# Retention's gates half by block products, retention in fewer VectorE instructions with its normalization a chunk later, and the order of the attention values' weight sums

## The chip, the cores and the metric

The kernel runs on one core of a Trainium2 chip. A core has a matrix engine (TensorE, PE in the profile; its weight loads are listed apart as PEld), VectorE (DVE), ScalarE (ACT), GpSimd (POOL) and SyncE (SP), which here only issues transfers. Each engine works through its own instructions in order; semaphores hold an instruction until what it needs is there. The metric is the device time of one execution in microseconds (us); of several runs the median counts.

## The reference

One decoder block on a sequence of 1024 tokens with 1024 channels, in float32. `h = modulate(rms_norm(x))` is projected by `w_in` to the queries, keys, values and gates of a retention branch (4 heads, 256 wide for queries and keys, 512 for values and gates), to the queries, keys and values of three groups of dilated attention, and to two merge gates. Retention goes through each head in chunks of 128 tokens:

```python
s = jnp.einsum('bhid,bhjd->bhij', qi, ki) * inner_decay[None]
o = (jnp.einsum('bhij,bhje->bhie', s, vi)
     + jnp.einsum('bhid,bhde->bhie', qi, state) * q_decay[None, :, :, None])
state = (state * chunk_decay[None, :, None, None]
         + jnp.einsum('bhjd,bhje->bhde', ki * k_decay[None, :, :, None], vi))
...
ro = ((ro - mu) * lax.rsqrt(var + GN_EPS)).transpose(0, 2, 1, 3).reshape(B, S, RET_V_W)
ro = (ro * gn_g.astype(jnp.float32) + gn_b.astype(jnp.float32)).astype(h.dtype)
ret_out = (jax.nn.silu(rg) * ro) @ w_ret_out
```

Then come the attention, the gated merge, `w_o`, a squared-ReLU MLP and a last norm. Six modulation vectors are made from `c` by `w_ada`.

## The kernel before, in words

**Arithmetic.** Each float32 operand is split into a high part (`hi`, a cast on ACT) and a low part (`lo`, the rest, a subtraction on DVE), and a product is three matmuls: low by high, high by low, high by high (`mm3`, L201, L203, L205). A full matmul has 128 x 128 weights and 512 moving columns.

**Plain and block products.** A plain projection of 128 output channels (`proj_mm`) goes over 8 blocks of input channels, 2 halves of the tokens and 3 matmuls: 48. A block product (`Blocks`, and by hand in `avb_mm` and `v_mm`) takes 256 output channels, both halves of the tokens and all input channels as a 2 x 2 matrix of blocks and needs seven products in place of eight, at the price of sums of weights and of results on DVE (L243, L1043) and copies on ACT. One such pair has 7 x 4 x 3 = 84 matmuls.

**Order of the work.** The order on every engine is the order in which the Python code issues (`manual_schedule`). Stages: the norm of the input; the attention's values (`av_first`, plain, and `av_blocks`, block products; its table `work` says what is issued behind which product); 18 pairs of block products (`queries_keys`, order `PAIRS`: r = retention's queries or keys, a = attention's queries, g = merge gates); retention's values (`values`, block products); retention; the attention of two pairs of heads; the merge; the MLP.

**Attention values' sums.** The sums s1, s2 and s4 of the weights are made in place in two tiles `AB["s", j]` by accumulating transfers that POOL issues (`avb_add`, L886). `avb_split` splits such a tile (ACT L914, DVE L916 or L918) and then issues the next sum into it. `avb_post` takes results out of PSUM (ACT L948, L951). `bias_out` (L440) spreads the attention's bias rows in DRAM, twelve stores on SP.

**Retention.** `chunk(h, c)` is called for 4 heads x 8 chunks (g = 8h + c) and does, in this order:
- SP fetches the queries, keys and values of chunk g + 3 (`fetch`).
- PE: the state's update `kv`, two tiles of 512 columns (not in chunk 7); then a part of the gate projection `rg` (16 blocks of 48 matmuls in the 32 chunks: 24 matmuls a chunk, 12 here and 12 below).
- DVE: state = state x decay + kv (L698; a copy, L696, in chunk 0), in two halves.
- `ahead(2)`: what the next chunk's loads need: a split of gate weights before every second chunk (ACT L191, DVE L192) and in every chunk one product of `w_ada` with c (DVE L452, L454), 32 in all.
- `s_kt(g + 1)`: PE makes the scores `sT` of the next chunk and transposes its keys; ACT L635 and DVE L636, L637 make `sm`, ACT L638 and DVE L639 split it, ACT L645 and DVE L646 make `kh` and `kl`, the keys for the next `kv`.
- PE: `o`, from the state's halves `sh`, `sl` (6 matmuls, not in chunk 0) and from scores and values (3).
- ACT L711 and DVE L712: the new state's halves, 512 columns at a time; ACT L612 and POOL L613 split queries and keys of chunk g + 2.
- PE: `on_T(g - 1)`, four transposes of the normalized output of the chunk before, which ACT (L658) copies out; the rest of the gate matmuls.
- DVE L722, L723, L724, POOL L725 (a power of -1/2), DVE L726, L728: mean, variance, and the normalized `o`.
- ACT L732, every second chunk: Silu of a gate block. In chunks 0 to 3, `u_final` finishes one block of 128 channels of the head before: ACT L667 twice, DVE L669 once, a store on SP.

[...]

Of the kernel before, what the change touches and what calls it, by code (L numbers as in the profile page):

```python
# [21 lines left out]
H = 4  # L22
# [18 lines left out]
CS_QD = 132  # L41
CS_QD2 = 136
# [92 lines left out]
def block_kernel(ctx, tc, io, stop=None, dbg=None):  # L135
# [535 lines left out]

    def chunk(h, c, ahead, w=None):
# [12 lines left out]
        kvs = []  # L685
# [8 lines left out]
        for i, kv in enumerate(kvs):  # L694
            if c == 0:
                nc.vector.tensor_copy(st[:, i, :], kv)  # L696
            else:
                nc.vector.scalar_tensor_tensor(st[:, i, :], st[:, i, :], float(GAMMA[h] ** C), kv,  # L698
                                               op0=ALU.mult, op1=ALU.add)
        ahead(2)  # L700
        if g + 1 < NG:
            s_kt(g + 1)
        po = ps_s(f"o{h}{c}")
# [5 lines left out]
        if c < NC - 1:  # L709
            for i in range(2):  # L710
                nc.scalar.copy(sh[:, i, :], st[:, i, :])  # L711
                nc.vector.tensor_sub(sl[:, i, :], st[:, i, :], fv(sh[:, i, :]))  # L712
# [11 lines left out]
        nc.vector.tensor_scalar(gr, ba[:, 1:2], ct[:, CS_QD2 + h:CS_QD2 + h + 1], GN_EPS, op0=ALU.mult, op1=ALU.add)  # L724
        nc.gpsimd.tensor_tensor(gr, gr, mhalf[:, 0:1], op=ALU.pow)  # L725
        nc.vector.tensor_mul(gr, gr, ct[:, CS_QD + h:CS_QD + h + 1])  # L726
        on = p.tile([P, DV], F32, tag="on", bufs=1, name=f"onm{h}{c}")
        nc.vector.tensor_scalar(on, po, ba[:, 0:1], gr, op0=ALU.subtract, op1=ALU.mult)  # L728
# [138 lines left out]
    def avb_tile(n, part, name):  # L867

        if n in (2, 6) or n > 11:
            return x4(name, F32R)  # L870
# [94 lines left out]
    def av_blocks(ahead):  # L965

        def tables():
# [32 lines left out]
    PAIRS = [{"r": r_pairs, "a": a_pairs, "g": g_pairs}[i].pop(0) for i in "rargrargrargrargaa"]  # L1000
# [3 lines left out]
    def a_load(q, part):  # L1004
        pair = PAIRS[q]
        src = io[{"g": "w_gate2", "a": "w_aq"}.get(pair[0]) or f"w_r{pair[1]}"]
# [19 lines left out]
    def a_out(q, n, x, y=None):  # L1026
# [12 lines left out]
        f = AF.Sigmoid if pair[0] == "g" else AF.Copy  # L1039
        if y is None:  # L1040
            nc.scalar.activation(o, view(x), f)
        else:
            (nc.vector.tensor_add if n == "12" else nc.vector.tensor_sub)(o, view(x), view(y))  # L1043
            if pair[0] == "g":
                nc.scalar.activation(o, o, f)
        if n in ("12", "21"):
            if pair[0] == "g":
                dst = gate_d[GATES[2 * pair[1] + i]]
            elif pair[0] == "a":
# [19 lines left out]

    gate_d = [dram.tile([P, S], F32, name=f"gated{i}") for i in range(16)]  # L1070
# [109 lines left out]

    def values(ahead):
# [1387 lines left out]
```

## Time and profile before

| | |
|---|---|
| median of 3 runs | 2232.15 us (2231.87 to 2234.04) |
| profiled execution | 2236.08 us |
| its span, first to last instruction | 2234.3 us |
| granted TensorE clock, mean | 0.993 |
| chain that ended last, PE's share | 86% |

The profile is of one execution. "Busy" is the time in which an engine had an instruction at work; PE's busy time is modelled, since matmuls are pipelined, so the distance between starts says more than a duration. The view of stretches gives the busy time of each engine in a window with the granted clock; the view of waits says which instruction waited, for whom, how long and how often; the timeline lists starts and durations, with the wait before an instruction and what ended it in brackets.

### The profile page before, as it was taken

How to read it: one execution, taken by the hardware profiler on the slowest of the kernel's cores; microseconds unless marked ns; L12 is line 12 of the kernel's file. 1: busy time of each engine (PE TensorE's matmuls, PEld its weight loads, DVE VectorE, ACT ScalarE, POOL GpSimd, SP SyncE). 2: the span in 40 equal slices, each digit the busy share in tenths (PEclk: the TensorE clock that was granted, in tenths of full speed). 3: DMA queues.
4: the chain of work that ended last, by engine and by line, in shares of the span. 5: the costliest groups of instructions: out<-in, count | busy, mean ns of one | idle time of the engine just before them, and what ended most of it. 6: DMA issues, size and time to landing. Idle time of an engine off the chain costs nothing.

```text
span 2234.3 us, 27105 instructions
## 1 busy us (share of the span) xinstructions
PE 2173.9 (97%) x10082; PEld 1799.7 (81%) x10082; DVE 1469.6 (66%) x2303; ACT 912.2 (41%) x1671; POOL 155.1 (7%) x176
## 2 busy tenths in 40 slices
PE   7999999999999999999999999999999999999998
PEld 5778888888877888888888788888778888788887
DVE  6657777754448778855554654676866665787845
ACT  4432332223334445544634633524444445433412
POOL 0100111000012122110000000002000000000003
PEclk9999999999999999999999999999999999999999
DMA  9859999724775556549723355654234444745322
GB/s 384 248 174 284 288 306 270 205 87 174 250 270 170 166 181 207 193 159 249 228 62 96 102 210 195 235 179 160 66 133 150 156 155 164 257 144 170 123 85 76
DMA packets 157602, 414.15 MB, mean 185 GB/s; under 512 B 27222, under 2 KB 55133, under 8 KB 153054
## 3 DMA queue, kind: packets, MB, share of 16 engines
q1 hardware_dynamic: 149598, 364.19, 46.6%
q0 software_dynamic: 7872, 48.24, 9.3%
q8 instruction: 79, 1.29, 0.2%
q14 instruction: 53, 0.43, 0.1%
HBM read 321.51 MB, written 156.13 MB: 214 GB/s over the span
## 4 chain that ended last, share of the span: by engine, by line
PE 86%; DVE 5%; ACT 2%; issue 1%; DMA 1%; POOL 0%; POOLq 0%; SPq 0%; DVEq 0%; ACTq 0%
PE qap L203 5%; PE qap L205 5%; PE qap L201 5%; PE fp L201 4%; PE fp L203 4%; PE fp L205 4%; PE rg L201 3%; PE rg L203 3%; PE rg L205 3%; PE f2a L203 2%; PE f2a L205 2%; PE f2a L201 2%; PE ak L201 2%; PE ak L203 2%; PE ak L205 2%; PE va L203 1%
## 5 line engine op out<-in xcount | busy, mean ns | idle before, releaser
L201 PE MATMUL qap<-hh,qaw 128*128 128x512 f32 x216 | 84.0, 389 | 0.0
L203 PE MATMUL qap<-hl,qaw 128*128 128x512 f32 x216 | 84.0, 389 | 0.0
L205 PE MATMUL qap<-hh,qaw 128*128 128x512 f32 x216 | 84.0, 389 | 0.0
L613 POOL TENSOR_TENSOR j<-qk,j 128x512 fp32r<-128x512 f32 x32 | 43.3, 1354 | 468.4 <-ACT j L612 446.4
L2028 ACT ACTIVATE a<-a 128x512 f32<-128x512 f32 x48 | 30.3, 632 | 79.5 <-DVE a L2027 79.5
L1925 POOL TENSOR_TENSOR accnf<-accnf,sqnf 128x256 f32<-128x256 f32 (+1 forms) x18 | 16.6, 921 | 620.7 <-ACT sqnf L1924 620.7
L1382 ACT ACTIVATE P<-P,ng 128x128 f32<-128x128 f32 (+1 forms) x96 | 41.9, 438 | 38.7 <-DVE ng L1379 38.7
L258 DVE TENSOR_TENSOR fw<-w1r,fw 128x512 fp32r<-128x512 f32 x48 | 33.0, 688 | 36.2 <-ACT fw L248 36.2
L2214 ACT CAST w2h<-w2s 128x512 fp32r<-128x512 f32 x36 | 22.4, 621 | 78.8 <-DVE w2s L2252 77.7
L635 ACT COPY sm<-sT 128x128 f32<-128x128 f32 x32 | 8.5, 265 | 103.9 <-PE sT L626 103.9
L201 PE MATMUL fp<-h2h,fw 128*128 128x512 f32 x128 | 50.0, 390 | 0.0
L203 PE MATMUL fp<-h2l,fw 128*128 128x512 f32 x128 | 49.8, 389 | 0.0
L205 PE MATMUL fp<-h2h,fw 128*128 128x512 f32 x128 | 49.8, 389 | 0.0
L201 PE MATMUL roa<-rh,rwl 128*128 128x512 f32 x128 | 49.8, 389 | 0.0
L203 PE MATMUL roa<-rl,rwh 128*128 128x512 f32 x128 | 49.8, 389 | 0.0
L205 PE MATMUL roa<-rh,rwh 128*128 128x512 f32 x128 | 49.8, 389 | 0.0
L1763 DVE TENSOR_TENSOR rwl<-rwl,rwh 128x1024 fp32r<-128x1024 f32 x25 | 30.2, 1220 | 29.1 <-ACT rwh L1793 29.1
L1925 POOL TENSOR_TENSOR accn<-accn,sqn 128x512 f32<-128x512 f32 x12 | 15.5, 1293 | 478.2 <-ACT sqn L1924 478.2
L201 PEld LDWEIGHTS qap<-hh,qaw 128*128 128x128 f32 x216 | 40.5, 188 | 8.5
L203 PEld LDWEIGHTS qap<-hl,qaw 128*128 128x128 f32 x216 | 40.6, 188 | 8.4
L205 PEld LDWEIGHTS qap<-hh,qaw 128*128 128x128 f32 x216 | 40.6, 188 | 8.3
L258 DVE TENSOR_TENSOR qaw<-wa,qaw 128x512 fp32r<-128x512 f32 x54 | 36.9, 685 | 7.5 <-ACT qaw L248 7.5
(3063 smaller groups left out, 7197.1 us busy)
## 6 DMA issues: line engine op xcount, KB each, us to landing
v<-vd SPq DMA_DIRECT2D x32, 512.0 KB, 4.8
raw<-in_w_ada_dram SPq DMA_DIRECT2D x32, 512.0 KB, 5.1
w1r<-in_w_ff_dram SPq DMA_DIRECT2D x32, 512.0 KB, 5.0
vd<-vo SPq DMA_DIRECT2D x24, 512.0 KB, 4.2
yt<-y POOLq DMA_DIRECT2D x6, 2048.0 KB, 15.4
xsd<-as SPq DMA_DIRECT2D x24, 512.0 KB, 2.8
w2r<-in_w_ff2s_dram SPq DMA_DIRECT2D x24, 512.0 KB, 7.1
em<-in_w_ada_dram SPq DMA_DIRECT2D x16, 512.0 KB, 10.2
```

What stands on the lines that cost most here:

```text
L201: nc.tensor.matmul(o, wl, xh, start=first, stop=False, skip_group_check=skip)
L203: nc.tensor.matmul(o, wh, xl, start=False, stop=False, skip_group_check=skip)
L205: nc.tensor.matmul(o, wh, xh, start=False, stop=last, skip_group_check=skip)
L258: nc.vector.tensor_sub(t[:, 512:], src, fv(t[:, :512]))
L613: nc.gpsimd.tensor_sub(t[:, 1], src, fv(t[:, 0]))
L635: nc.scalar.copy(sm, ps[:, :C])
L1382: nc.scalar.activation(v, v, AF.Exp, bias=ng[:, blk:blk + 1], accum_out=st[:, g, blk, 2 + a:3 + a])
L1763: nc.vector.tensor_sub(lo, fv(lo), fv(hi))
L1925: (nc.vector if f == 7 else nc.gpsimd).tensor_add(G["acc", key], G["acc", key], sq)
L2028: nc.scalar.activation(o, o, AF.Relu)
L2214: nc.scalar.copy(hi, src)
```

## The change: what it does

1. Of each head's four gate blocks two are still projected inside retention (12 matmuls a chunk); the other two are a pair of block products among the `queries_keys` pairs (s in `PAIRS`, now 22 pairs, the merge gates last), with Silu, stored to DRAM (`srg_d`) and fetched in chunks 4 and 5.
2. In retention, `kv` is one double tile and the state's update, high and low half are one instruction each on 1024 columns. The query decay is taken out of the normalization (its epsilon is scaled by a table), and `o` is normalized by ACT with a scale and a bias, one chunk later (`normed(g - 1)`, behind `s_kt`). The transposes come two chunks later than `o` and stand between the gate matmuls and the scores. `u_final` moves to chunks 2 to 5.
3. Thirteen of the 32 `w_ada` products move from retention to `values` (`v_mod`).
4. In `av_blocks` the splits of s1 stand one to two products earlier, the first in tiles of another ring, and `bias_out` moves to `queries_keys`.

```diff
+    def normed(g):
+
+        h, c = divmod(g, NC)
+        po, ba, gr = hd["o", h, c]
+        nb = R["p"].tile([P, 1], F32, tag="nb", bufs=2, name=f"nb{h}{c}")
+        nc.vector.scalar_tensor_tensor(nb, ba[:, 0:1], -1.0, gr, op0=ALU.mult, op1=ALU.mult)
+        on = R["p"].tile([P, DV], F32, tag="on", bufs=2, name=f"onm{h}{c}")
+        nc.scalar.activation(on, po, AF.Identity, scale=gr, bias=nb)
+        hd["o", h, c] = on
...
-        if c % 2 == 0:
+        if c % 4 == 0:
             hd["rgw"] = w
             hd["rgp"] = ps_mm(f"rg{h}{c}")
-        ks = range(4 * (c % 2), 4 * (c % 2) + 4)
+        if c in (4, 5):
+            hd["srg", h, c - 2] = etile(f"srg{h}{c - 2}")
+            nc.sync.dma_start(hd["srg", h, c - 2], srg_d[h][c - 4])
+        ks = range(2 * (c % 4), 2 * (c % 4) + 2)
...
+            kv = ps_mm(f"kv{h}{c}")
             for i in range(2):
-                kv = ps_s(f"kv{h}{c}{i}")
-                mm3([kv], (kh[:, i, :], kl[:, i, :]), [(vh, vl)], True, True)
-                kvs.append(kv)
+                mm3([kv[:, i]], (kh[:, i, :], kl[:, i, :]), [(vh, vl)], True, True)
         if g > 0:
-            proj_mm(hd["rgp"], hd["rgw"], ks[:2])
...
+            proj_mm(hd["rgp"], hd["rgw"], ks[:1])
+        if g > 1:
+            on_T(*divmod(g - 2, NC))
+        if c == 0:
+            nc.vector.tensor_copy(flat(st), flat(kv))
+        elif c < NC - 1:
+            nc.vector.scalar_tensor_tensor(flat(st), flat(st), float(GAMMA[h] ** C), flat(kv),
+                                           op0=ALU.mult, op1=ALU.add)
         ahead(2)
         if g + 1 < NG:
             s_kt(g + 1)
+        if g > 0:
+            normed(g - 1)
         po = ps_s(f"o{h}{c}")
...
-            for i in range(2):
-                nc.scalar.copy(sh[:, i, :], st[:, i, :])
-                nc.vector.tensor_sub(sl[:, i, :], st[:, i, :], fv(sh[:, i, :]))
+            nc.scalar.copy(flat(sh), flat(st))
+            nc.vector.tensor_sub(flat(sl), flat(st), fv(flat(sh)))
         if g + 2 < NG:
             jit_qk(g + 2)
         if g > 0:
-            on_T(*divmod(g - 1, NC))
-        if g > 0:
-            proj_mm(hd["rgp"], hd["rgw"], ks[2:])
+            proj_mm(hd["rgp"], hd["rgw"], ks[1:])
...
-        nc.vector.tensor_scalar(gr, ba[:, 1:2], ct[:, CS_QD2 + h:CS_QD2 + h + 1], GN_EPS, op0=ALU.mult, op1=ALU.add)
+        nc.vector.tensor_add(gr, ba[:, 1:2], ct[:, CS_EPS + h:CS_EPS + h + 1])
         nc.gpsimd.tensor_tensor(gr, gr, mhalf[:, 0:1], op=ALU.pow)
-        nc.vector.tensor_mul(gr, gr, ct[:, CS_QD + h:CS_QD + h + 1])
-        on = p.tile([P, DV], F32, tag="on", bufs=1, name=f"onm{h}{c}")
-        nc.vector.tensor_scalar(on, po, ba[:, 0:1], gr, op0=ALU.subtract, op1=ALU.mult)
-        hd["o", h, c] = on
-        if c % 2 == 1:
-            hd["srg", h, c // 2] = etile(f"srg{h}{c // 2}")
-            nc.scalar.activation(hd["srg", h, c // 2], flat(hd["rgp"]), AF.Silu)
-        if h > 0 and c < 4:
-            u_final(h - 1, (c,))
+        hd["o", h, c] = po, ba, gr
+        if c % 4 == 3:
+            hd["srg", h, c // 4] = etile(f"srg{h}{c // 4}")
+            nc.scalar.activation(hd["srg", h, c // 4], flat(hd["rgp"]), AF.Silu)
+        if h > 0 and 1 < c < 6:
+            u_final(h - 1, (c - 2,))
...
-        if n in (2, 6) or n > 11:
+        if n in (2, 4, 6) or n > 11:
             return x4(name, F32R)
...
-                (0, 1): [lambda: sums_of_h("t1")], (0, 2): [lambda: bias_out(0)],
-                (0, 3): [lambda: sums_of_h("t3"), lambda: bias_out(1)],
-                (1, 0): [lambda: avb_split(2, 0), lambda: bias_out(2)], (1, 1): [lambda: avb_split(2, 1)],
+                (0, 1): [lambda: sums_of_h("t1")], (0, 2): [lambda: avb_split(2, 0)],
+                (0, 3): [lambda: sums_of_h("t3")], (1, 0): [lambda: avb_split(2, 1)],
...
-    PAIRS = [{"r": r_pairs, "a": a_pairs, "g": g_pairs}[i].pop(0) for i in "rargrargrargrargaa"]
+    s_pairs = [("s", h) for h in range(H)]
+    PAIRS = [{"r": r_pairs, "a": a_pairs, "g": g_pairs, "s": s_pairs}[i].pop(0) for i in "rsrarsrarsrarsraggagga"]
...
-            if pair[0] == "g":
+            if pair[0] in "gs":
                 nc.scalar.activation(o, o, f)
...
+            if n == "11" and 0 < q < 4:
+                bias_out(q - 1)
...
+    def v_mod(i):
+
+        t, j = cs[:, i % 2], VMODS[i]
+        nc.vector.scalar_tensor_tensor(t, t, 1.0, cb, op0=ALU.mult, op1=ALU.mult, accum_out=mods[:, j:j + 1])
+        nc.vector.tensor_add(mods[:, j:j + 1], mods[:, j:j + 1], vec[:, VC_BADA + j:VC_BADA + j + 1])
...
+            if i < last:
+                nc.sync.dma_start(cs[:, i % 2], io["w_ada"][VMODS[i]])
...
+                if p == 3 and i > 0:
+                    v_mod(i - 1)
...
-                      ([wsplit(io["w_rg"][4 * h + c // 2])] if c % 2 == 0 else []) + [mod_load(later_mods[8 * h + c])],
-                      manual=True)
+                      ([wsplit(io["w_rg"][2 * h + c // 4])] if c % 4 == 0 else []) +
+                      ([mod_load(later_mods.pop(0))] if c in ((1, 2, 3, 5, 6) if h < 3 else (1, 3, 5, 6)) else []), manual=True)
...
+                normed(NG - 1)
                 for _ in range(4):
                     next(gen)
+                on_T(H - 1, NC - 2)
                 on_T(H - 1, NC - 1)
```

More of the change, by code (lines that the diff above doesn't have):

```diff
@@ L40 @@
 CS_KDEC = 128
-CS_QD = 132
-CS_QD2 = 136
+CS_EPS = 132
 CS_ONE = 140
@@ L1038, in a_out @@
             view = lambda z: z.rearrange("p (i r) -> p r i", r=8)
-        f = AF.Sigmoid if pair[0] == "g" else AF.Copy
+        f = {"g": AF.Sigmoid, "s": AF.Silu}.get(pair[0], AF.Copy)
         if y is None:
@@ L1048, in a_out @@
                 dst = gate_d[GATES[2 * pair[1] + i]]
+            elif pair[0] == "s":
+                dst = srg_d[pair[1]][i]
             elif pair[0] == "a":
@@ L1068, in rotate @@
             nc.sync.dma_start(qk_d[h][:, 2 * (t == "k") + i], OA[q][i])
+    srg_d = [[dram.tile([P, S], F32, name=f"srgd{h}{i}") for i in range(2)] for h in range(H)]
     gate_d = [dram.tile([P, S], F32, name=f"gated{i}") for i in range(16)]
@@ L1179, in v_post @@
         nc.sync.dma_start(v_d[2 * hp + int(blk[0]) - 1][:, p + 4 * (int(blk[1]) - 1)], fv(t))
+    later_mods = [G1 + k for k in range(NK)] + [SH2 + k for k in range(NK)] + \
+                 [SC2 + k for k in range(NK)] + [G2 + k for k in range(NK)]
+    def v_mod(i):
+        t, j = cs[:, i % 2], VMODS[i]
+        nc.vector.scalar_tensor_tensor(t, t, 1.0, cb, op0=ALU.mult, op1=ALU.mult, accum_out=mods[:, j:j + 1])
+        nc.vector.tensor_add(mods[:, j:j + 1], mods[:, j:j + 1], vec[:, VC_BADA + j:VC_BADA + j + 1])
+    VMODS = [later_mods.pop(0) for _ in range(len(VSEQ) - 1)]
     def values(ahead):
@@ L1223, in block_kernel @@
     steps.add(queries_keys, manual=True)
-    later_mods = [G1 + k for k in range(NK)] + [SH2 + k for k in range(NK)] + \
-                 [SC2 + k for k in range(NK)] + [G2 + k for k in range(NK)]
     for h in range(H):
```

16 lines of the change are left out of this document (5 added, 11 removed).

## The prediction, made before the change was run

> **What bounds the kernel now.** I began with the shares of the page: TensorE (PE) is at work nearly all the time, so a change pays only if it takes matmuls away or ends one of PE's few waits, and it costs as soon as it gives PE a new one.
>
> ```profile
> span 2234.3 us, 27105 instructions
> PE 2173.9 (97%) x10082; PEld 1799.7 (81%) x10082; DVE 1469.6 (66%) x2303; ACT 912.2 (41%) x1671; POOL 155.1 (7%) x176
> ```
>
> Next the view by stretches for the stages that the edits touch: the queries, keys and gates by block products (158.8 to 501.5 us), the values (to 657.8) and retention (to 976.7). The first three columns are the stretch, its length and PE's busy time with its instructions; VectorE (DVE) stands fourth after the length's PE and PEld.
>
> ```profile
> 158.80:501.50 342.70, 342.70 (x1514) 283.85 (x1512) 244.29 (x383) 100.18 (x171) 33.65 (x48) 1.00 0.78 243
> 501.50:657.80 156.30, 154.23 (x674) 127.23 (x672) 73.28 (x87) 60.15 (x84) 7.11 (x10) 0.99 0.62 219
> 657.80:976.70 318.90, 313.12 (x1510) 259.79 (x1509) 247.82 (x519) 142.68 (x359) 57.91 (x62) 0.99 0.55 183
> ```
>
> In the block products PE never stops: 342.70/1512 = 0.2267 us a matmul of 512 columns. In retention it stops only at the start; the view of waits has two PE rows there:
>
> ```profile
> PE rg L201 <- DVE kl L646: 3.3, 1, 3.3
> PE kv L201 <- DVE kl L646: 2.5, 1, 2.5
> ```
>
> So retention's 32 chunks are bound by PE, and the next question is how closely DVE follows. The timeline of DVE for one round of a chunk that also finishes a block of the head before (starts, durations):
>
> ```profile
> 767.42 1.28 DVE L698 SCALAR_TENSOR_TENSOR state<-state,kv 128x512 f32<-128x512 f32 x2
> 768.62 1.22 DVE L452 SCALAR_TENSOR_TENSOR raw<-raw,cb 128x1024 f32<-128x1024 f32 x1
> ...
> 769.96 0.28 DVE L636 TENSOR_TENSOR sm<-sm,sT 128x128 f32<-128x128 f32 x1
> 770.27 0.29 DVE L637 TENSOR_TENSOR sm<-sm,decay 128x128 f32<-128x128 f32 x1
> 770.93 0.29 DVE L639 TENSOR_TENSOR sml<-sm,smh 128x128 fp32r<-128x128 f32 x1 [0.36 <-ACT smh L638]
> 771.30 0.48 DVE L646 SCALAR_TENSOR_TENSOR kl<-kT,ct,kh 128x256 fp32r<-128x256 f32 x1
> 771.81 1.29 DVE L712 TENSOR_TENSOR statel<-state,stateh 128x512 fp32r<-128x512 f32 x2
> 773.02 0.69 DVE L722 BATCH_NORM_STATS2 bn<-o 128x6 f32<-128x512 f32 x1
> 773.75 0.18 DVE L723 BATCH_NORM_AGGREGATE ba<-bn 128x2 f32<-128x6 f32 x1
> 773.97 0.21 DVE L724 TENSOR_SCALAR gr<-ba,ct 128x1 f32<-128x1 f32 x1
> 774.83 0.16 DVE L726 TENSOR_TENSOR gr<-gr,ct 128x1 f32<-128x1 f32 x1 [0.65 <-POOL gr L725]
> 775.10 0.81 DVE L728 TENSOR_SCALAR onm<-o,ba,gr 128x512 f32<-128x512 f32 x1
> 775.82 1.22 DVE L669 TENSOR_TENSOR on<-on,srg 128x1024 f32<-128x1024 f32 x1
> 776.96 1.28 DVE L698 SCALAR_TENSOR_TENSOR state<-state,kv 128x512 f32<-128x512 f32 x2
> ```
>
> ```profile
> 768.16 0.51 PE L201 MATMUL o<-stateh,j 128*128 128x512 f32 x1
> ...
> 778.19 0.48 PE L201 MATMUL o<-stateh,j 128*128 128x512 f32 x1
> ```
>
> DVE's round takes 776.96 - 767.42 = 9.54 us, PE's 778.19 - 768.16 = 10.03. DVE is hidden by half a microsecond. That is the number to keep in mind.
>
> **The change part by part. Matmuls.** Retention's gates (rg) are 16 blocks of 48 matmuls, 768. Half of them stay, 384; the other half become four pairs of block products with 7 x 12 = 84 matmuls each, 336. 48 matmuls go: 48 x 0.2267 = **-10.9 us**, provided PE stays without waits in both stages. In the block stage it should: 384 x 0.2267 = 87.0 us leave retention and 76.2 us arrive where DVE is busy 244.29 of 342.70 us; a new pair has the same sums, splits and outputs as a gate pair, with Silu for Sigmoid, and gate pairs stall nothing now. Its extra weights (1 MB a pair) and its stores come at the same rate per pair as today's.
>
> **Moved modulation products.** Thirteen of retention's 32 (L452, with its small followers 769.96 - 768.62 = 1.34 us of DVE) move to the values: 17.4 us more beside 73.28 of 156.30. Hidden by matmuls of 10.9 us a step; SP gets thirteen loads into a table that nobody reads any more. Only the last one stands near a wait, the 3.3 us before the first rg; without cover it costs 1.3. I take 0. The bias rows' twelve stores go to places behind block products, where PE has no wait: 0.
>
> **Attention values' sums.** The stretch 105 to 130 us is where PE now loses time before retention:
>
> ```profile
> 105.00:130.00 25.00, 18.82 (x69) 14.44 (x68) 10.11 (x13) 10.28 (x16) 2.44 (x2) 0.86 0.74 186
> ```
>
> 25.00 - 69 x 0.2267 = 9.4 us lost, in two places. PE stops at 110.51 and again at 119.10; POOL's accumulating transfers and ScalarE (ACT) say why:
>
> ```profile
> 79.51 1.23 POOL L886 DMA_DIRECT2D abs<-in_w_av_dram  x1 [6.77 <-DMA abs<-in_w_av_dram]
> 92.83 1.21 POOL L886 DMA_DIRECT2D abs<-in_w_av_dram  x1 [12.09 <-DVE abl L916]
> 102.98 1.22 POOL L886 DMA_DIRECT2D abs<-in_w_av_dram  x1 [8.93 <-DMA abs<-in_w_av_dram]
> 111.83 1.21 POOL L886 DMA_DIRECT2D abs<-in_w_av_dram  x1 [7.63 <-DMA abs<-in_w_av_dram]
> ```
>
> ```profile
> 111.59 1.06 ACT L914 ACTIVATE abh<-abs 128x1024 fp32r<-128x1024 f32 x1 [7.79 <-DMA abs<-in_w_av_dram]
> ...
> 122.47 2.04 ACT L948 COPY abr<-ava 128x512 f32<-128x512 f32 x4
> ```
>
> The transfers follow one another, each after the landing of the last, 8 to 10 us apart. The one at 92.83 waited for the split of s1, which the change puts in front; then it starts when 79.51's has landed, some 88.1, and the next at 96.7 to 98.2, landing at 105.3 to 107.4 and not at 111.5. PE needs it at 110.5: the first stop (3.1 us) goes. The second is the copy of 122.47 at the end of ACT's line that begins with 111.59; that line moves up 4.1 to 6.2 us, PE only 3.1, so 0.9 to 3.0 us of it stay, and with 3.0 the slow matmuls after it. Gain 3.8 to 8.5: I take **-6 us**; if the order of the transfers binds elsewhere, 0.
>
> **Retention.** A chunk loses 12 matmuls: PE's round falls to 10.03 - 2.72 = 7.31 us, in chunk 0 of a head (three matmuls for o and not nine) 5.95, in chunk 7 (no kv) about 5.95. DVE's round, in the new order, with starts from the rows above: state in one instruction (like L452 and L669: 1.14 to the next start), modulation 1.34, sm 0.31, decay and the wait for smh 0.66, sml 0.37, kl 0.40. Now comes what is new: nb (like L726, 0.16) lets ACT normalize o of the chunk before, and the state's high half stands behind that on ACT, and its low half on DVE waits for it. The nearest rows for these two on ACT, the Identity with scale and bias on 512 columns and a 1024 cast:
>
> ```profile
> 770.60 0.30 ACT L638 CAST smh<-sm 128x128 fp32r<-128x128 f32 x1 [2.31 <-DVE sm L637]
> ...
> 771.17 1.13 ACT L711 CAST stateh<-state 128x512 fp32r<-128x512 f32 x2
> 772.20 0.63 ACT L612 CAST j<-qk 128x512 fp32r<-128x512 f32 x1
> ...
> 773.35 1.55 ACT L667 ACTIVATE on<-on,gnt 128x512 f32<-128x512 f32 x2
> 774.77 1.06 ACT L191 CAST raw_5772h<-raw 128x1024 fp32r<-128x1024 f32 x1
> ```
>
> The Identity comes to (774.77 - 773.35)/2 = 0.71 us, and from one engine to the other go 0.03 (ACT ends smh at 770.90, DVE's sml starts at 770.93). So from nb to the low half 0.16 + 0.71 + 1.06 + 2 x 0.03 = 1.99 us, in which DVE stands still. Then low half 1.14, bn 0.73, aggregate 0.22, add 0.10, and the block's product 1.14 where there is one. The sum is 9.54 us with it and 8.40 without. **DVE's round stays what it was**: what goes (the pow's wait, a multiply, the 512-column subtract, together 775.82 - 773.97 = 1.85) comes back as the wait for ACT, since halves that overlapped became one copy and one subtract. Against PE's 7.31 it is now the longer one, and PE must wait for kl and sm.
>
> Chunks 0 to 5 of heads 1 to 3: 2 x 8.40 + 3 x 9.54 + 9.34 (chunk 3 has a split, 1.14, for the modulation) = 54.8, PE 5.95 + 5 x 7.31 = 42.5: 12.3 us too late. Chunks 6 (no modulation, no kl: some 6.4 against 7.1) and 7 (no state: 4.2 against 5.95) give 2.4 back: 9.9 a head, 29.7 for three. Head 0 has no products: 50.1 - 42.5 - 2.4 = 5.2, of which the 2.5 us wait in chunk 1 stands already: 2.7. To these 32 come the starts of a gate tile (chunks 0 and 4): its first matmul takes the banks that Silu reads, and Silu stands on ACT behind normalization, state copy and jit copy: kl's end + some 3.5 us, while PE arrives 1.4 after it. 2 us at seven places, but DVE catches up meanwhile; I take 5. **+37 us.** Bounds: if half of the 1.99 were hidden, 24 rounds (chunks 0 to 5 of four heads) would lose 1 us each, 13; if each of some 45 stops costs PE 0.15 more to start again and nothing of Silu's wait is caught up, 37 + 7 + 6 = 50.
>
> **The sum**: -10.9 - 6 + 37 = +20 us on the profiled execution's 2236.1 us (1.8 above its span), or 2256. The median of the runs is 2232.15, 3.9 lower; the forecast for it is **2252 us**.
>
> **The rivals.** *Faster: DVE's round fits.* The decisive point is 7.3 us per round. For it: per chunk DVE loses three instructions and some 2.5 us of busy time, busy alone would be under 7. Against: the order is fixed, and in it nothing is ready for DVE while ACT normalizes and copies. If it fits, 2232.15 - 10.9 - 6 = 2215 us. [...]
>
> *Slower still: PE's clock.* A stop costs more if the clock drops after it:
>
> ```profile
> 501.49 0.39 PE L201 MATMUL va<-vwh,hl 128*128 128x512 f32 x1
> 503.95 0.50 PE L203 MATMUL va<-vwlFalse,hh 128*128 128x512 f32 x1 [2.07 <-DVE vwlFalse L1136]
> ...
> 505.14 0.63 PE L205 MATMUL va<-vwh,hh 128*128 128x512 f32 x1
> 505.57 0.63 PE L201 MATMUL va<-vwh,hl 128*128 128x512 f32 x1
> ```
>
> 2.46 us between two starts, and soon after it they come every 0.43 us, 0.20 too slow, for some eight to thirteen matmuls: 1.6 to 2.6 us a time. The stop at 110.51 (2.2 us) was not followed by it. My stops are 0.5 to 2 us; were the seven at gate tiles longer (if kv, which comes first in the chunk, took the banks that Silu reads, each would grow by kv's and the six matmuls' 1.4), they would add 11 to 18: 2263 to 2270, with the upper bound of the stops up to 2285. [...]
>
> *No difference*: stops of about 17 us would cancel the gains, 2232. *The sums' order does nothing*: 2258, within the forecast's range.
>
> **How the numbers follow.** Forecast (PE waits for DVE's and ACT's rounds in retention) 0.75, its own range 2238 to 2268: -10.9, less 8.5 or 3.8, plus 25 (midway to the lower bound) or 50. Clock 0.07; no difference 0.06; faster 0.12. 0.2%, or 4.5 us, is about what a measurement of this kernel can tell from no change. The range goes down to 2227, where the lower bound of the stops, 13, leads (-10.9 - 8.5 + 13), and up to 2269; it leaves out the faster case and most of the clock's, 0.19. Faster by over 0.2%: 0.13; within: 0.08; slower: 0.79.
>
> **What would show it.** Right: PE rows "kv <- DVE kl", "sT" or "rg <- ACT srg" in the waits of retention, many and short; DVE's low half of the state (now one 1024 subtract) with a wait for ACT's copy in each chunk; a retention stage of 318.9 - 87.0 + 37 = 269 us, a block stage of 419 us with PE busy throughout, and 105 to 130 us with most of its gaps gone. Wrong: retention of some 232 us without PE waits (then DVE's order leaves more free than I read), or PE waits in the block stage or the values, which I priced at nothing.

## The result and the profile after

The kernel after takes 2265.72 us (median of 4 runs, 2264.78 to 2266.97) and the kernel before, on the same chip, 2233.1 (2231.87 to 2235.14). The ratio is 1.0142, with a 95% interval of 1.0129 to 1.0155: 32.6 us slower. The forecast was 2252, its range 2227 to 2269. The profiled execution took 2264.78 us, 28.7 more than the one of before; the medians lie 32.6 apart, since before's profiled execution was 3.0 above its median and this one 0.9 below.

The view by stretches has the stages at their new places (length, then PE, PEld, DVE, ACT and POOL busy): the front where PE lost time, the block stage, the values, retention, and 240 us of the attention.

```profile
105.00:130.00 25.00, 25.00 (x112) 20.70 (x111) 16.70 (x21) 13.64 (x21) 1.73 (x2) 1.00 0.65 179
149.20:569.70 420.50, 419.22 (x1850) 346.77 (x1848) 286.57 (x447) 128.56 (x219) 33.62 (x48) 1.00 0.70 224
569.70:726.00 156.30, 154.23 (x674) 127.20 (x673) 87.19 (x121) 59.40 (x84) 8.01 (x10) 0.99 0.73 260
726.00:1001.60 275.60, 238.80 (x1122) 188.35 (x1121) 191.68 (x388) 148.09 (x342) 77.64 (x61) 0.98 0.56 186
1001.60:1241.80 240.20, 234.25 (x1261) 199.19 (x1260) 126.97 (x183) 116.76 (x274) 7.44 (x9) 1.00 0.59 171
```

Against before: the block stage begins at 149.2 and not at 158.8 (-9.6); it is 77.8 longer; the values keep their 156.3; retention falls by 43.3, while 87.0 us of matmuls left it, so **43.7 us of new idling** stand there; from retention's end to the end of the span it is 2262.9 - 1001.6 = 1261.3 us where it was 1257.6 (+3.7). -9.6 + 77.8 - 43.3 + 3.7 = +28.6.

The waits within retention, of PE and DVE:

```profile
DVE statel L724 <- ACT stateh L723: 48.6, 28, 1.8
...
PE sT L623 <- POOL j L612: 14.4, 18, 1.7
PE kv L200 <- DVE kl L645: 8.5, 9, 3.1
...
PE rg L200 <- ACT srg L739: 8.3, 5, 3.0
```

PE now waits many times, for three different engines, and in no row for more than a third of the 43.7. Such a list names the last of several that were late, not the bound. DVE's timeline over one round of a chunk shows more:

```profile
816.51 1.23 DVE L724 TENSOR_TENSOR statel<-state,stateh 128x1024 fp32r<-128x1024 f32 x1 [1.78 <-ACT stateh L723]
...
822.24 0.29 DVE L638 TENSOR_TENSOR sml<-sm,smh 128x128 fp32r<-128x128 f32 x1 [0.36 <-ACT smh L637]
...
823.02 0.15 DVE L676 SCALAR_TENSOR_TENSOR nb<-ba,gr 128x1 f32<-128x1 f32 x1
824.95 1.23 DVE L724 TENSOR_TENSOR statel<-state,stateh 128x1024 fp32r<-128x1024 f32 x1 [1.78 <-ACT stateh L723]
```

824.95 - 816.51 = 8.44 us, forecast 8.40. From `nb` to the low half it is 824.95 - 823.02 = 1.93 us, forecast 1.99, and 1.78 of that is a stop. DVE has no other stop in this round but the 0.36.

The experiments start from this **theory**: VectorE works through its line in order, and its round, ScalarE's copy included, is longer than TensorE's 7.31. **Rivals**: GpSimd's low half of `j` is the bound (the longest PE row); the new order itself does the harm, whatever PE's round; ScalarE's line of copies is the bound and VectorE's stop only slack.

### The profile page after: what moved, and what is told of

It reads as the page before. It is cut to its first block, busy times and chain, and to the rows that moved or that the text cites. A ratio compares the mean times of both kernels' runs of the same rounds, so it can differ in the third digit from the quotient of the medians.

```text
span 2262.9 us, 27026 instructions
## 1 busy us (share of the span) xinstructions
PE 2175.3 (96%) x10034; PEld 1791.5 (79%) x10034; DVE 1470.0 (65%) x2271; ACT 947.6 (42%) x1707; POOL 176.3 (8%) x176
## 4 chain that ended last, share of the span: by engine, by line
PE 76%; DVE 11%; ACT 5%; DMA 5%; issue 2%; POOL 0%; SPq 0%; POOLq 0%; DVEq 0%; ACTq 0%
PE qap L200 6%; PE qap L204 6%; PE qap L202 6%; PE fp L200 4%; PE fp L204 4%; PE fp L202 4%; PE f2a L202 2%; PE f2a L204 2%; PE f2a L200 2%; PE ak L200 1%; PE ak L202 1%; PE ak L204 1%; PE va L202 1%; PE va L204 1%; PE va L200 1%
## 5 line engine op out<-in xcount | busy, mean ns | idle before, releaser
L200 PE MATMUL qap<-hh,qaw 128*128 128x512 f32 x264 | 102.8, 389 | 1.3 <-DVE qat L284 1.3
L204 PE MATMUL qap<-hh,qaw 128*128 128x512 f32 x264 | 102.7, 389 | 0.0
L202 PE MATMUL qap<-hl,qaw 128*128 128x512 f32 x264 | 102.7, 389 | 0.0
L612 POOL TENSOR_TENSOR j<-qk,j 128x512 fp32r<-128x512 f32 x32 | 54.8, 1714 | 473.9 <-ACT j L611 467.9
L724 DVE TENSOR_TENSOR statel<-state,stateh 128x1024 fp32r<-128x1024 f32 x28 | 34.3, 1226 | 48.6 <-ACT stateh L723 48.6
L200 PEld LDWEIGHTS qap<-hh,qaw 128*128 128x128 f32 x264 | 49.6, 188 | 11.9 <-DVE qat L284 1.7
L257 DVE TENSOR_TENSOR qaw<-wa,qaw 128x512 fp32r<-128x512 f32 x66 | 45.1, 686 | 20.0 <-ACT qaw L247 20.0
L202 PEld LDWEIGHTS qap<-hl,qaw 128*128 128x128 f32 x264 | 49.6, 188 | 10.3
L204 PEld LDWEIGHTS qap<-hh,qaw 128*128 128x128 f32 x264 | 49.5, 188 | 10.3
L247 ACT CAST qaw<-wa 128x512 fp32r<-128x512 f32 x66 | 39.7, 617 | 32.0 <-PE qap L204 21.8
```

The lines of the kernel that those rows point to most:

```text
L200: nc.tensor.matmul(o, wl, xh, start=first, stop=False, skip_group_check=skip)
L202: nc.tensor.matmul(o, wh, xl, start=False, stop=False, skip_group_check=skip)
L204: nc.tensor.matmul(o, wh, xh, start=False, stop=last, skip_group_check=skip)
L247: nc.scalar.copy(t[:, :512], src)
L257: nc.vector.tensor_sub(t[:, 512:], src, fv(t[:, :512]))
L612: nc.gpsimd.tensor_sub(t[:, 1], src, fv(t[:, 0]))
```

## The experiments

### Old order, new gates; and new order, old gates

First the two halves of the change apart. Retention's gates half by block products, but `chunk` as it was, with the gates' new strides:

```diff
-            kv = ps_mm(f"kv{h}{c}")
+                kv = ps_s(f"kv{h}{c}{i}")
...
-        if g > 0:
-            normed(g - 1)
...
+        nc.vector.tensor_scalar(on, po, ba[:, 0:1], gr, op0=ALU.subtract, op1=ALU.mult)
```

> The kernel after with before's order and operations of a chunk (state in halves, normalization by VectorE in the same chunk), the gates half by block products as in after. Theory (VectorE's in-order round of 8.4 to 9.54 us bounds retention as soon as TensorE's round falls to 7.31, in either order): about the kernel after, 2266 us, 2260 to 2272. Rival (the new order does the harm, its copy of the whole state and the late normalization): retention near 319 - 87 = 232 us, the whole near 2232 - 9.6 - 9.3 + 3.7 = 2217 us.

Measured: 2253.9 us, ratio to before 1.0085 (1.0070 to 1.0100). DVE's timeline, from one state update to the next:

```profile
804.08 1.28 DVE L701 SCALAR_TENSOR_TENSOR state<-state,kv 128x512 f32<-128x512 f32 x2
...
811.50 0.16 DVE L729 TENSOR_TENSOR gr<-gr,ct 128x1 f32<-128x1 f32 x1 [0.66 <-POOL gr L728]
...
812.49 1.22 DVE L669 TENSOR_TENSOR on<-on,srg 128x1024 f32<-128x1024 f32 x1
813.62 1.28 DVE L701 SCALAR_TENSOR_TENSOR state<-state,kv 128x512 f32<-128x512 f32 x2
```

813.62 - 804.08 = 9.54 us, what the same line took in before. There PE's 10.03 hid it; now it is retention's pace. So in the old order the new gates, with the moved products and the sums' order that this kernel keeps, already lose more than they save: 20 us slower than before. But the kernel after is 11.8 us slower still, which the theory, at 2260 to 2272, did not hold. By the two traces 6.4 of that are in retention (275.6 us against 269.25), and of these 6.0 in head 0, here

```profile
732.52:795.33 62.81, 57.45 (x274) 46.38 (x273) 51.68 (x117) 28.10 (x78) 15.12 (x16) 0.97 0.59 191
```

and 68.78 us in the kernel after. Head 1 takes nearly the same in both orders, 67.4 and 68.3 us. The rest is outside retention: 1.6 in the block stage, 1.6 in the values, 2.2 behind retention.

The other half: before, with the new order of a chunk, and the finished blocks in chunks 1 to 4.

```diff
+            kv = ps_mm(f"kv{h}{c}")
...
+        if g > 1:
+            on_T(*divmod(g - 2, NC))
...
+        if g > 0:
+            normed(g - 1)
...
-        if h > 0 and c < 4:
-            u_final(h - 1, (c,))
+        if h > 0 and 0 < c < 5:
+            u_final(h - 1, (c - 1,))
```

> The kernel before with after's order and operations of a chunk, all gates as plain matmuls in retention and all 32 modulations there. Theory: TensorE's round is 10.03 us again, VectorE's 9.54 is hidden, so about the kernel before: 2233 us, 2229 to 2240 (sixteen gate tiles wait on Silu). Rival (the new order does the harm): 2233 + 30 = 2263 us.

Measured: 2276.34 us, ratio 1.0184 (1.0169 to 1.0199), 43 us slower than before. **The theory failed here**; VectorE, with fewer instructions, is not hidden behind PE's long round. ACT's and DVE's timelines of this kernel, at a chunk that prepares the next gate weights, show a wait that the theory did not have:

```profile
835.18 0.77 ACT L657 COPY on<-oT 128x128 f32<-128x128 f32 x4 [3.85 <-PE oT L655]
835.82 1.08 ACT L190 CAST raw_6157h<-raw 128x1024 fp32r<-128x1024 f32 x1
```

```profile
836.93 1.23 DVE L191 TENSOR_TENSOR raw_6157l<-raw,raw_6157h 128x1024 fp32r<-128x1024 f32 x1 [3.69 <-ACT raw_6157h L190]
...
840.76 0.48 DVE L645 SCALAR_TENSOR_TENSOR kl<-kT,ct,kh 128x256 fp32r<-128x256 f32 x1
```

The transposes of `on` stand behind the gate matmuls on PE; ACT, which has their copies next, waits 3.85 us for them; the weights' cast stands behind those copies, DVE waits 3.69 for the cast, and only then come `sm` and `kl`, for which PE's next `kv` waits. The wait goes round three engines. It repeats once per gate tile, and the tiles are twice as many here as in the kernel after, where DVE waits for such a cast three times in retention, 1.5 us in all. PE's largest row here is another one:

```profile
PE rg L200 <- ACT srg L737: 21.2, 15, 1.7
```

The first matmul of a gate tile waits for Silu, which stands on ACT behind the normalization, and that waits for `nb`, behind `kl` on DVE. How the 43 us divide between the two waits was not tried apart.

### Which wait in the round

`j`'s copy ahead of the state's:

```diff
+        if g + 2 < NG:
+            jit_qk(g + 2)
         if c < NC - 1:
             nc.scalar.copy(flat(sh), flat(st))
             nc.vector.tensor_sub(flat(sl), flat(st), fv(flat(sh)))
-        if g + 2 < NG:
-            jit_qk(g + 2)
```

> The kernel after with the copy of j on ScalarE ahead of the copy of the state. Theory (VectorE's round, with its wait for ScalarE's copy of the state, is the bound): VectorE waits 0.5 us more a round, 24 rounds, +12: 2278 us. Rival (GpSimd's low half of j bounds the round, since TensorE's longest row of waits, 14.4 us in 18, is sT for j): those waits go, 2266 - 14 = 2252 us.

Measured: 2277.8 us, ratio 1.0186 (1.0170 to 1.0202). GpSimd as the bound is out: PE's waits for `j` fell to 3.4 us, and the time rose by the theory's 12. In retention's waits:

```profile
DVE statel L726 <- ACT stateh L725: 62.6, 28, 2.3
...
PE sT L623 <- POOL j L612: 3.4, 3, 1.3
```

Then the opposite, VectorE's stop made shorter: the normalization behind the state's split.

```diff
-        if g > 0:
-            normed(g - 1)
         po = ps_s(f"o{h}{c}")
...
             nc.vector.tensor_sub(flat(sl), flat(st), fv(flat(sh)))
+        if g > 0:
+            normed(g - 1)
```

> The kernel after with the normalization of the chunk before (nb, onm) put behind the state's split. Theory (VectorE's round with its 1.8 us wait for ScalarE's state copy is the bound): the wait falls to some 0.6 us, the round from 8.44 to 7.3, then TensorE's 7.31 is as long; some 20 rounds, -20: 2246 us, 2240 to 2252. Rival (the loop that binds runs from sT over ScalarE's four copies of on and sm to kl and the next kv, and VectorE's wait is only slack in it): 2266 us, within 4.

Measured: 2266.63 us, ratio 1.0140 (1.0125 to 1.0156): no change against the kernel after, which is the rival's number. Retention's waits:

```profile
DVE on L668 <- ACT on L666: 23.8, 12, 2.7
DVE statel L722 <- ACT stateh L721: 15.8, 28, 1.0
```

The stop went from 48.6 to 15.8 us, as the theory wanted, and the plain rounds shrank (chunk 1 of head 1 from 8.43 us to 7.84). But `on`, the finished block, which had waited 1.4 us in the kernel after, now waits 23.8: its two scalings on ACT stand behind the normalization. The rounds with a block or a weight split grew (chunk 3: 10.72 to 11.42; chunks 6 and 7 together: 15.55 to 17.77). So VectorE's round binds the plain chunks, as their 7.84 shows. That ScalarE's line binds the loaded ones, and a wait moved along that line comes out elsewhere, is read from these waits and was not tried by itself.

### The modulation products taken out

Two a step in the values, six left in chunks 6 and 7 of retention:

```diff
-    VMODS = [later_mods.pop(0) for _ in range(len(VSEQ) - 1)]
+    VMODS = [later_mods.pop(0) for _ in range(2 * (len(VSEQ) - 1))]
...
-                      ([mod_load(later_mods.pop(0))] if c in ((1, 2, 3, 5, 6) if h < 3 else (1, 3, 5, 6)) else []), manual=True)
+                      ([mod_load(later_mods.pop(0))] if c in ((7,) if h < 2 else (0, 7)) else []), manual=True)
```

> The kernel after with 26 modulation products in the values (two a step) and the other six in chunks 6 and 7 of retention. Theory (VectorE's round is the bound): 1.34 us less in each of the 19 rounds that had one, of which a few are bound by TensorE already: -15 to -25, 2241 to 2251 us, and the values keep their 156.3 us. Rival (the loop over ScalarE binds): 2266 us, within 4.

Measured: 2260.74 us, ratio 1.0121 (1.0107 to 1.0135): between the two. The plain rounds fell to 7.7, but the values did not stay free: DVE waited there for the products' late loads (6.5 us in three waits), and PE's first gate matmul for DVE.

```profile
PE rg L200 <- DVE sm L635: 11.0, 1, 11.0
```

That row was 2.3 in the kernel after. And the two places in chunks 6 and 7 that I took for free cost some 2 us each. Next, the normalization behind the state's split and these moved products together, with one Silu of a single column at the end of the values:

```diff
+        nc.scalar.activation(pad[:, :1], ct[:, CS_ONE:CS_ONE + 1], AF.Silu)
```

> Both of these together, and one Silu of a single column at the end of the values, so that its table is loaded there. Theory: VectorE's round is 8.44 - 1.2 - 1.3 = 5.9 us, TensorE's 7.31 the longer one; retention near 236 to 242 us, the whole 2222 to 2232 us. Rival (the loop over ScalarE): 2258 to 2266 us.

Measured: 2271.39 us, ratio 1.0168 (1.0154 to 1.0181): slower than the kernel after, so the theory failed. The plain rounds stayed at 7.7, the start was as late as in the kernel before this one (12.2 us), chunks 3, 6 and 7 of head 1 took 11.4, 9.8 and 9.5 us, and the mean granted clock fell to 0.989 (0.992 in the kernel after). What each of these took was not tried apart.

So the products were placed anew: 13 in the values as in after, 19 in the last pairs of the block stage. (In this kernel and in the first of the next part, the products' loads may overwrite the rotation's table before its last use, so one head's keys come out changed; the work is the same.)

```diff
+    def block_mod(s):
+        if s >= 0 and s % 2 == 0 and s // 2 < len(BMODS):
+            nc.sync.dma_start(cs[:, s // 2 % 2], io["w_ada"][BMODS[s // 2]])
+        m = (s - 3) // 2
+        if s >= 3 and s % 2 and m < len(BMODS):
+            mod_prep(BMODS[m])(cs[:, m % 2])
```

> The kernel after with no modulation product in retention: 13 stay in the values as in after, the other 19 go to the last six pairs of the block stage, through the table of the rotation, which is free by then. Theory (VectorE's round binds the plain chunks, 8.43 to 7.7 us as in the kernel with the modulations in the values, whose late start of retention, 8.7 us, and whose two products in chunks 6 and 7, some 2 us each, do not come here): 2260.7 - 8.7 - 7 = 2245 us, 2240 to 2250. Rival (ScalarE's line of copies, normalization, state and j binds the chunks with a gate product or a weight split, so that only the plain ones gain): 2254 to 2260 us.

Measured: 2247.31 us, ratio 1.0054 (1.0038 to 1.0069), 18.4 less than the kernel after, as the theory said. Retention, and one of PE's waits in it:

```profile
727.95:986.85 258.90, 234.31 (x1122) 187.10 (x1121) 167.89 (x331) 148.71 (x342) 77.52 (x61) 0.99 0.50 159
```

```profile
PE o L200 <- ACT on L657: 3.3, 15, 0.2
```

Retention is 16.7 us shorter than in the kernel after: that much of the 43.7 goes with these products. The block stage pays 3.7 of it back (424.2 us and not 420.5). The plain rounds stop at 7.7 and not at PE's 7.31; DVE's line is shorter there (8.44 less the product's 1.34), and PE has one stop of some 0.4 us between starts, its wait for ACT's copies of the transposes.

### VectorE made shorter than TensorE, in the old order

The same with the old order of a chunk, the finished blocks in every second chunk, the stored gates fetched one chunk later, and the Silu of one column:

```diff
-        if h > 0 and c < 4:
-            u_final(h - 1, (c,))
+        if h > 0 and c % 2 == 0:
+            u_final(h - 1, (c // 2,))
```

> The kernel with before's order of a chunk on the new gates, with no modulation product in retention (as in the kernel beside this one), the four finished gate blocks of a head in chunks 0, 2, 4, 6 of the next and not 0 to 3, and the Silu of one column at the end of the values. Theory (in this order VectorE's round is the only bound: 9.54 - 1.34 = 8.20 us with a block's product, 8.40 - 1.34 = 7.06 without, against TensorE's 7.31): heads 1 and 2 fall from 67.4 to some 60.6, head 0 from 62.8 to 57, in all -26: 2254 - 26 = 2228 us, 2222 to 2234, so just faster than before. Rival (TensorE's waits for the state and for onm, 14 and 10 us in that kernel, do not go with the modulations): 2240 to 2246 us.

Measured: 2234.34 us, ratio 0.9995 (0.9986 to 1.0003). The heads are as forecast (57.0, 60.8, 60.9 us); the total lacks some 6 us, of which one wait in the attention, `sc` for DVE's `kl`, is 2.3. Rounds with a finished block still last 8.1 to 8.2. Last, that block's product on GpSimd, with two of the modulation products back in retention, at the ends of heads 1 and 2:

```diff
-            nc.vector.tensor_mul(t, t, hd["srg", h, e])
+            (nc.gpsimd if h < H - 1 else nc.vector).tensor_tensor(t, t, hd["srg", h, e], op=ALU.mult)
```

> The kernel with before's order of a chunk, new gates and no modulations in retention's rounds, with the finished block's product (on times srg) on GpSimd and not on VectorE while retention runs. Two of the modulations stand at the ends of heads 1 and 2, the others in the block stage and the values. In the two kernels before this one, the first modulations of the block stage could overwrite the rotation's table before its last use, so that one head's keys came out changed at the same amount of work; here they start five steps later. Theory (VectorE's round was the only bound of the rounds of 8.1 to 8.2 us; without the product it is 7.06, TensorE's 7.31 binds): heads 1 and 2 from 60.8 to some 56.5, head 3 from 52.5 to 49, so 2234.3 - 12 = 2222 us, 2217 to 2227, 0.4% to 0.7% faster than before. Rival (GpSimd's product takes 3 us and holds up its pow, on which VectorE waits, and VectorE's subtracts slow GpSimd): rounds stay at 8 us, 2232 to 2238 us.

Measured: 2226.91 us, ratio to before 0.9970 (0.9959 to 0.9982): **faster than the kernel before** by 0.3%, the only one of these kernels that is clearly so. DVE's normalizations, then GpSimd's line, of this kernel:

```profile
798.23 0.81 DVE L731 TENSOR_SCALAR onm<-o,ba,gr 128x512 f32<-128x512 f32 x1
805.30 0.81 DVE L731 TENSOR_SCALAR onm<-o,ba,gr 128x512 f32<-128x512 f32 x1
812.49 0.81 DVE L731 TENSOR_SCALAR onm<-o,ba,gr 128x512 f32<-128x512 f32 x1
```

```profile
797.39 0.54 POOL L728 TENSOR_TENSOR gr<-gr,ct 128x1 f32<-128x1 f32 x1
798.11 2.37 POOL L669 TENSOR_TENSOR on<-on,srg 128x1024 f32<-128x1024 f32 x1 [0.18 <-ACT on L667]
803.10 1.36 POOL L613 TENSOR_TENSOR j<-qk,j 128x512 fp32r<-128x512 f32 x1 [2.62 <-ACT j L612]
```

The product takes 2.37 us and is over before `j` and the next pow; VectorE's rounds are 7.1 to 7.2, and PE's 7.3 leads again. Chunks 0 to 5 of head 1 in the kernel after and in this one:

```profile
804.25:856.95 52.70, 45.16 (x215) 35.04 (x215) 37.95 (x76) 30.48 (x70) 15.30 (x12) 1.00 0.55 184
```

```profile
792.73:836.85 44.12, 43.14 (x218) 35.54 (x216) 35.65 (x79) 25.05 (x68) 18.59 (x15) 1.00 0.46 150
```

### The order of the sums

Part four of the change alone, on the kernel before:

```diff
-        if n in (2, 6) or n > 11:
+        if n in (2, 4, 6) or n > 11:
             return x4(name, F32R)
...
-                (0, 1): [lambda: sums_of_h("t1")], (0, 2): [lambda: bias_out(0)],
-                (0, 3): [lambda: sums_of_h("t3"), lambda: bias_out(1)],
-                (1, 0): [lambda: avb_split(2, 0), lambda: bias_out(2)], (1, 1): [lambda: avb_split(2, 1)],
+                (0, 1): [lambda: sums_of_h("t1")], (0, 2): [lambda: avb_split(2, 0)],
+                (0, 3): [lambda: sums_of_h("t3")], (1, 0): [lambda: avb_split(2, 1)],
```

> The kernel before with the new order of the attention values' sums alone. Theory (the parts add up, and the front's gain of 158.77 - 149.21 = 9.6 us in the two traces belongs to the sums' order): 2233 - 9.6 = 2223.5 us. Rival (the front gains only 6, as I priced it, and the rest came with the new order of the pairs): 2227 us.

Measured: 2232.4 us, ratio 0.9994 (0.9984 to 1.0004): nothing, against both expectations. The front did gain its 9.6 us (the block stage begins at 149.2), but retention's start gave most of them back. ACT's and PE's waits there:

```profile
ACT sm L635 <- DMA vd<-vr: 7.0, 1, 7.0
```

```profile
PE rg L201 <- DVE kl L646: 9.9, 1, 9.9
```

PE's row was 3.3 in before, and ACT had no such wait. The new order needs two more tiles of the ring of large tiles; retention's small tiles are laid over that ring, and with the ring turned by two, `sm` lies under a value tile whose store has just been issued. To test this, the split stayed in the weight buffers:

```diff
-        if n in (2, 4, 6) or n > 11:
+        if n in (2, 6) or n > 11:
```

> The sums' order alone, but the split of the first sum stays in the weight buffers of before, so that the ring of large tiles turns as in before. Theory (in the sums-only kernel the front's 9.6 us were lost again at retention's start, because the ring had turned by two tiles and ScalarE's first sm waited 7.0 us for a store that reads the tile under it): now the store under sm is an older one, retention starts 9 us earlier, 2233 - 9 = 2224 us. Rival (retention's start is held by something else that comes at a fixed time, such as the reload of hh): 2232 us again.

Measured: 2231.55 us, ratio 0.9993 (0.9984 to 1.0002). The DMA wait is gone and PE's row is 3.3 again, so the ring as the cause of that wait is shown; but the front gained only 4.2 us now, since the split waits for its buffers, and the median moves by 2.4, which its interval doesn't tell from nothing. Last, the old order of the sums, with its tiles, put back into the kernel after:

```diff
-        if n in (2, 4, 6) or n > 11:
+        if n in (2, 6) or n > 11:
...
-                (0, 1): [lambda: sums_of_h("t1")], (0, 2): [lambda: avb_split(2, 0)],
-                (0, 3): [lambda: sums_of_h("t3")], (1, 0): [lambda: avb_split(2, 1)],
+                (0, 1): [lambda: sums_of_h("t1")], (0, 2): [lambda: bias_out(0)],
+                (0, 3): [lambda: sums_of_h("t3"), lambda: bias_out(1)],
+                (1, 0): [lambda: avb_split(2, 0), lambda: bias_out(2)], (1, 1): [lambda: avb_split(2, 1)],
```

> The kernel after with before's order of the attention values' sums (and before's places for the bias rows' stores). Theory (here the front's 9.6 us are carried to the end, since retention's first gate waits for DMAs whose start moves with the front): 2266 + 9.6 = 2275 us. Rival (a later wait swallows them, as it did in the two kernels with the sums' order alone): 2264 to 2268 us.

Measured: 2275.94 us, ratio 1.0183 (1.0169 to 1.0198), the theory's number, but not for its reason alone:

```profile
ACT sm L634 <- DMA vd<-vr: 7.2, 1, 7.2
```

Here the old order turns the ring to the bad place, as this wait shows. What the sums' order is worth by itself, between 1 and 10 us, is not separated.

## Why the prediction was right in sign, point by point

- **Matmuls, -10.9.** Right but for 1.6: 87.0 left and 77.8 came, 76.2 forecast. The rest is one stop of 1.67 us in the block stage, where the prediction had none; the old-order kernel, with the same pairs, has 418.9 us there, -10.8.
- **Moved products and stores in the values, 0.** Right: 156.3 as before. That there is room for 13 and not for 26 showed in the kernel with two a step.
- **The sums, -6 (3.8 to 8.5).** Mis-sized: 9.6 at the block stage's start, since the second stop went too (105 to 130 us now has PE busy throughout). That the gain arrives at the end hangs on the ring of buffers, which the prediction did not look at.
- **Retention, +37 (13 to 50).** It is 43.7, and the mechanism holds. DVE's plain round was to be 8.40 and is 8.44. DVE's state updates of chunks 2 to 6 of head 1 in the kernel after:

```profile
818.81 1.21 DVE L709 SCALAR_TENSOR_TENSOR state<-state,kv 128x1024 f32<-128x1024 f32 x1
828.38 1.21 DVE L709 SCALAR_TENSOR_TENSOR state<-state,kv 128x1024 f32<-128x1024 f32 x1
838.31 1.21 DVE L709 SCALAR_TENSOR_TENSOR state<-state,kv 128x1024 f32<-128x1024 f32 x1
847.89 1.21 DVE L709 SCALAR_TENSOR_TENSOR state<-state,kv 128x1024 f32<-128x1024 f32 x1
857.46 1.21 DVE L709 SCALAR_TENSOR_TENSOR state<-state,kv 128x1024 f32<-128x1024 f32 x1
```

  The rounds of chunks 2, 4 and 5, with a block's product, take 9.57, 9.58 and 9.57 (forecast 9.54), that of chunk 3, with a split in place of the modulation, 9.93 (forecast 9.34; `on` waits 0.46 of it for ACT, which has a Silu ahead of it). And taking work out of DVE's line paid: 16.7 us of retention by the modulations, 2234.3 to 2226.9 us by the products (0.9995 and 0.9970 of the kernel before). The term that was mis-sized is the account per head. Chunks 0 to 5 of heads 1 and 2: forecast 54.8 us, measured 52.7, mostly because chunk 0 takes PE 6.9 us and not DVE's 8.40. Chunks 6 and 7: the prediction let them **give 2.4 us back**, but they take 15.55 where PE needs 7.31 + 5.95 = 13.26, so they cost 2.3. PE's long wait there is this one:

```profile
PE sT L623 <- POOL j L612: 1.7, 1, 1.7
```

  The copy of `j` stands on ACT behind the normalization and the state's copy, and these follow DVE's `nb`: what DVE is late with after chunk 5 still holds PE in chunk 6. Modulations have no part in it, since the kernel without them takes 15.54 for the two. Head 0, forecast 5.2 late with 2.7 of it new, is 13 late:

```profile
735.47:804.25 68.78, 60.21 (x276) 48.07 (x274) 46.66 (x97) 33.37 (x79) 17.92 (x16) 0.93 0.54 177
```

  68.78 against 2 x 5.95 + 6 x 7.31 = 55.8. (Before, head 0 took 78.44; 96 matmuls or 21.8 us left it, so 12.1 are new.) Part of it is the first Silu, whose table load PE had not had to wait for before (there it takes 1.28 us at 685.62, and PE is busy throughout 685 to 690). ACT's and PE's timelines of the kernel after:

```profile
766.16 1.28 ACT L739 ACT_TABLE_LOAD   x1
767.46 1.02 ACT L739 ACTIVATE srg<-rg 128x1024 f32<-128x1024 f32 x1
```

```profile
765.13 0.39 PE L204 MATMUL kv<-v,kh 128*128 128x512 f32 x1
768.53 1.22 PE L200 MATMUL rg<-hh,raw_5459l 128*128 128x512 f32 x2 [3.01 <-ACT srg L739]
769.55 1.05 PE L202 MATMUL rg<-hl,raw_5459h 128*128 128x512 f32 x2
```

  3.40 us without a start, and slow matmuls after it (the granted clock is 0.50 from 767.83 to 774.65): the round is 13.1 us where the same chunk of the later heads takes 10.7. Where the rest of head 0's loss comes from is open.
- **What the order costs.** The prediction held the new order for neutral (9.54 and 8.40 in either). By the traces that is nearly so from head 1 on (head 1 takes 68.3 us in the new order, 67.4 in the old on the same gates); of the 11.8 us between the two kernels head 0 has 6.0. The wait from PE's transposes over ACT to DVE's weight split, shown for the kernel with old gates, is not what makes the kernel after's chunk 3 last 10.7 us: DVE's split starts there without a wait, and PE has another,

```profile
829.51 1.21 DVE L191 TENSOR_TENSOR raw_6095l<-raw,raw_6095h 128x1024 fp32r<-128x1024 f32 x1
```

```profile
835.78 0.73 PE L200 MATMUL rg<-hh,raw_6095l 128*128 128x512 f32 x2 [1.60 <-ACT srg L739]
```

  besides 0.84 us for `kl`. The first is the start of a gate tile, which the prediction had put at 2 us a place and 5 in all; the row of these waits above has 8.3.
- **After retention, +3.7.** Not priced. 1.2 of it is in the attention's first 239 us; the cause of the rest is open. From the attention's first scores to the end the fourteen traces take 1241.8 to 1247.9 us, before 1242.2 and after 1245.5, so the difference is no larger than others between these kernels.
- **The sum.** +20 forecast, +28.6 in the traces: the sums gave 3.6 us more, retention cost 6.7 more, the block stage 1.6 and the end 3.7. That the time fell within the range owes something to the first, which has nothing to do with retention.
- **The rivals.** "VectorE's round fits" was the condition that failed, and the last kernel shows what it is worth: with the round under 7.3 the time is 2226.9, not the rival's 2215. In its trace retention takes 241.6 us where 318.9 - 87.0 = 231.9 would be left: the two late modulation products take some 2 us each (chunks 6 and 7 of head 1: 15.36 for 13.26), chunk 3 of each head 0.8; the rest is not divided. The clock as a second loss is small: it fell to 0.50 after three of retention's stops, for 3.41, 3.41 and 6.82 us, and two of these, at the start (2.58 and 3.46 us), have their like in before (3.53 and 2.92 us, with 3.41 us at 0.50 after each); only the 3.40 us one is new.

## What to carry to other kernels

Before taking matmuls out of a stage, write down the in-order round of each other engine there, its waits for its neighbours included; the one that was hidden by half a microsecond sets the new pace, and the saving ends there. Fewer instructions do not shorten a round if what replaces them makes two engines wait for each other; work that belongs to no round (here the modulations) should leave it first. And a new tile in a ring of buffers moves every later tile of the ring: look at what lies over it hundreds of microseconds on.

## What the runs showed of the hardware

**Of two overlapping subtracts of VectorE and GpSimd, the later one took longer.** GpSimd's subtract for `j` takes 1.36 us in the rows above of the kernel with the product on GpSimd. In the kernel after it begins while VectorE's 1024-column `statel` (816.51 to 817.74) is at work:

```profile
817.13 1.74 POOL L612 TENSOR_TENSOR j<-qk,j 128x512 fp32r<-128x512 f32 x1 [6.00 <-ACT j L611]
```

With `j` ahead of the state, GpSimd begins first, and VectorE is the slower one, 1.54 us instead of 1.23:

```profile
815.03 1.30 POOL L612 TENSOR_TENSOR j<-qk,j 128x512 fp32r<-128x512 f32 x1 [5.05 <-issue]
```

```profile
815.88 1.54 DVE L726 TENSOR_TENSOR statel<-state,stateh 128x1024 fp32r<-128x1024 f32 x1 [2.30 <-ACT stateh L725]
```

In both cases the one that began second is the slower one. The losses, 0.4 and 0.3 us, are shorter than what the other still had to run (817.74 - 817.13 = 0.61 and 816.33 - 815.88 = 0.45), so a wait for the other's end is not shown; what slows the second one is open.

**The same stop does or does not lower the clock.** At the values' start PE goes without a start for 2.46 us in before (from 501.49), 2.45 in the kernel after (569.67) and 2.46 in the one with the old order (568.17). In the first two the granted clock is 0.50 for 3.41 us soon afterwards (504.78 to 508.19, 573.26 to 576.67), and matmuls come every 0.43 us; in the third they come every 0.23 until 572.34, where that timeline ends, and the values last 154.7 us, not 156.3 as in the kernel after. The length of a stop alone does not tell it either: after the 2.20 us at 110.51 in before the clock is 1.00 up to 119; after two stops in a row of 1.48 us each, at 1631.07 and 1633.11 in the kernel after, it is 0.50 from 1634.81 to 1638.22. With one trace of each kernel, it is open whether the same kernel would do it every time.
